# Layer 0's gated MLP: the seven-product form moves from the down projection to the up projection

## The chip, the cores and the metric

The kernel runs on one core of a Trainium2 chip. TensorE (PE in the profile) multiplies matrices into PSUM, which has eight banks of 128 x 512 float32. VectorE (DVE), ScalarE (ACT) and GpSimd (POOL) do the elementwise work; SyncE (SP) issues most of the loads. The metric is the device time in microseconds, the median of several runs; besides there is one profiled execution with its trace.

## The reference

Two decoder layers on 512 tokens of width 1024, all in float32. Layer 0 mixes tokens by causal pooling, layer 1 by sliding-window attention; each mixer is followed by a gated MLP with a causal convolution of width 3, and each has an RMS norm ahead of it. What matters here is the MLP of layer 0, with D_FF = 2816:

```python
def conv_glu_ffn(h, w_in, conv_w, conv_b, w_out):
    u = h @ w_in
    c = lax.conv_general_dilated(u, conv_w[:, None, :].astype(u.dtype), ..., feature_group_count=2 * D_FF) + conv_b
    a, g = c[..., :D_FF], c[..., D_FF:]
    return (a * jax.nn.silu(g)) @ w_out

hn = rms_norm(h, norm_ffn[i])
h = h + conv_glu_ffn(hn, ffn_w_in[i], ffn_conv_w[i], ffn_conv_b[i], ffn_w_out[i])
```

## The kernel before, in words

Activations lie with channels on partitions and tokens along the row: `h` is eight tiles of 128 x 512, and D_FF is 22 tiles of 128 channels. Every float32 product is made of three: each operand is split into a high part (a rounded copy, by ACT, line 99 for weights) and a low part (the rest, a subtraction on DVE, line 102), and `mm3` (lines 85 to 87) adds high x high, high x low and low x high in one bank. Weights come by `fetch` (line 91) into a `raw` tile (3 buffers) and are split into `wh` and `wl` tiles (4 buffers each).

The MLP of layer 0 is `mlp(fp, 0, ...)`, followed by `mlp_out`.

- Up (`mlp_in`): for each channel tile j and each s (1 is the gate g, 0 the value a), eight weight tiles of 128 x 128 times `xs` (the scaled `h` with the norm's gain, not yet its root) give one bank. There are six banks in this ring (`ps`) and two in the other (`aux`). The root of the norm is known late: the squares of `h` are added by `norm.add` (line 216, on POOL), `stats` multiplies by ones (line 222), `rsqrt_mean` finds the root on DVE, and `spread` brings it across partitions (line 233) into `rb` (line 236). So the first output tiles wait in their banks.
- `conv_chunk`: DVE multiplies the bank by `rb` into `c_u` (line 359), ACT makes the first tap with the bias (line 362), and two shifted adds follow on DVE (lines 363 and 364). The gate gets its Silu on ACT (line 402), and line 411 multiplies.
- Down: the 22 channel tiles are 11 pairs, in groups of 4, 4 and 3. The first two groups use a form with seven products for a 2 x 2 block product instead of eight (Winograd's variant of Strassen's): the blocks are the two channel tiles of a pair, two output tiles, and the two halves of 256 tokens. `split_sum` makes seven sums of the activations per pair; `sum_weights` makes seven weight tiles out of four, called R (two as loaded), Q (one as loaded), U (two sums, which an accumulating DMA from POOL's queue makes, line 460) and W (two further sums by POOL, lines 463 and 464); `mlp_sums` runs four rounds of seven products per group. A product is four channel tiles times three matmuls of 256 columns, so a round is 84 matmuls; it copies a bank's half out by ACT between two products (lines 483 and 487). The third group is plain (`mlp_out`): six channel tiles, three matmuls of 512 columns each, for each of eight output tiles; `after` then makes the scaled input of the attention and the squares for its norm.

The order on each engine is fixed when the program is built. A planner walks through the program with its own estimates of durations: on each engine it places, of what is ready, the instruction that stands first in program order. `pin` keeps chosen instructions in program order. Engines then run their lists in order, and waits are inserted where one needs another's result or a buffer.

Of the kernel before, what the change touches and what calls it, by code (L numbers as in the profile page):

```python
# [19 lines left out]
F32 = mybir.dt.float32  # L20
# [6 lines left out]
P = 128  # L27
D = 1024
# [8 lines left out]
GROUPS = (((4, True), (4, True), (3, False)), ((4, True), (4, True), (3, False)))  # L37
# [21 lines left out]
def trunk(ctx: ExitStack, tc: tile.TileContext, x_tok, x_t, vecs, w_pool, w_kq, w_v, w_o, w_in, gain, w_out, w_sums, w_tok, out):  # L59
# [48 lines left out]
    def in_weights(layer, j, s, eng=None, raw=None, pin=lambda ins: ins):  # L108
        return weights(w_in[layer, j, s], D, f"wi{layer}_{j}_{s}", eng, raw, 256 if eng else 1024, pin)

    def out_weights(layer, m):
        n = 2 * GROUPS[layer][-1][0]
        w = weights(w_out[layer][m], n * P, f"wo{layer}_{m}")
        return [part(w, k) for k in range(n)]
# [133 lines left out]
    def pool_mixer(norm, xs, ws):  # L248
# [59 lines left out]
        for i, (j, t) in enumerate(pre[:3]):  # L308
# [3 lines left out]
            raws.append(fetch(w_in[0, j, t], D, f"wi0_{j}_{t}"))  # L312
# [39 lines left out]
        for c in range(NC):  # L352
            norm.add(c)


# [11 lines left out]
    def mlp_in(fp, layer, xs, norm, ws0, z, turns):  # L367

        pairs = [k for n, k in GROUPS[layer] for _ in range(n)]
# [8 lines left out]
        for n, sums in GROUPS[layer]:  # L378
            first += 2 * n
            stops.add(min(first - 1 + sums, NF - 1))  # L380
# [67 lines left out]
    def sum_weights(fp, layer, g, p, n):  # L448

        src = w_sums[layer][g][p]  # L450
        w = n * P
        name = f"ws{layer}_{g}_{p}"
        v = fp.tile([P, 1024], F32, tag="uv", name=f"{name}_u_raw", bufs=4)
        u, v = v, fp.tile([P, 1024], F32, tag="uv", name=f"{name}_v_raw", bufs=4)
        r = wp.tile([P, 1024], F32, tag="raw", name=f"{name}_r_raw", bufs=3)
        q = wp.tile([P, 1024], F32, tag="raw", name=f"{name}_q_raw", bufs=3)
        nc.sync.dma_start(u[:, : 2 * w].rearrange("p (a b) -> p a b", a=2), src[:, 0:4:2, :])
        nc.sync.dma_start(r[:, : 2 * w].rearrange("p (a b) -> p a b", a=2), src[:, 0:2, :])
        nc.sync.dma_start(q[:, :w], src[:, 3, :])
        pin(G.dma_start(u[:, : 2 * w].rearrange("p (a b) -> p a b", a=2), src[:, 2:4, :], accum_op=ALU.add))  # L460
        R = weights(None, 2 * w, f"{name}_r", raw=r)
        Q = weights(None, w, f"{name}_q", raw=q)
# [590 lines left out]
```

## Time and profile before

| | us |
|---|---|
| runs before: median of 3 (lowest to highest) | 907.51 (907.15 to 907.55) |
| the profiled execution's own time | 907.31 |
| its span, first to last instruction | 905.6 |
| TensorE busy in the span | 895.2 |
| VectorE busy in the span | 683.2 |
| ScalarE busy in the span | 453.7 |
| GpSimd busy in the span | 192.3 |

The profile shows one execution. A row of its groups names the line, the engine, the operation, the output and inputs by the program's names, the shape and the count, then the busy time, the mean duration of one in ns, and the idle time of the engine before them with what ended most of it. A row of the timeline gives the start and the duration in us. Consecutive instructions of an engine overlap by their latency, so what one of them holds the engine for is the distance from start to start. A string of 40 digits shows the busy share in tenths, one for each fortieth of the span.

### The profile page before, as it was taken

The page shows a single profiled execution, that of the slowest core. Times are in us where ns is not written, and L with a number is a line of the kernel's source. Part 1 is how long each engine was busy: PE and PEld are TensorE (multiplying, and loading weights), DVE is VectorE, ACT ScalarE, POOL GpSimd, SP SyncE. Part 2 cuts the span into 40 slices and gives each one's busy share as a digit, 9 for nine tenths or more (in the row PEclk, how much of TensorE's full clock was granted, in tenths as well). Part 3 has the DMA queues.
Part 4 walks back from the last instruction along what each step waited for, and adds up shares of the span by engine and source line. Part 5 has one row for each costly group of instructions (what it writes and reads, how often), then busy time and mean ns, then how long its engine had stood idle before and what let it go on. Part 6 is the DMA issues. An engine that isn't in the chain of part 4 may idle for free.

```text
span 905.6 us, 12207 instructions
## 1 busy us (share of the span) xinstructions
PE 895.2 (99%) x4560; PEld 764.0 (84%) x4560; DVE 683.2 (75%) x1066; ACT 453.7 (50%) x697; POOL 192.3 (21%) x265
## 2 busy tenths in 40 slices
PE   9999999999999999999999999999999999999996
PEld 8888889888899888888889888888888888888885
DVE  7689998688987676555887381998976888966744
ACT  7755454444454344535888352654433444534434
POOL 3810123000321000425765040000230002300004
PEclk9999999999999999999999999999999999999999
DMA  8342536423444323322110041338286221453202
GB/s 321 114 139 93 152 86 189 134 98 106 122 116 134 124 69 93 117 94 93 48 47 24 1 162 48 117 122 227 48 219 197 94 93 47 93 173 107 93 24 93
DMA packets 30748, 101.29 MB, mean 112 GB/s; under 512 B 3296, under 2 KB 3296, under 8 KB 30688
## 3 DMA queue, kind: packets, MB, share of 16 engines
q1 hardware_dynamic: 28384, 92.11, 30.4%
q0 software_dynamic: 2304, 8.39, 5.5%
q8 instruction: 36, 0.59, 0.3%
q14 instruction: 24, 0.20, 0.1%
HBM read 98.39 MB, written 2.10 MB: 111 GB/s over the span
## 4 chain that ended last, share of the span: by engine, by line
PE 92%; POOL 3%; ACT 2%; DVE 1%; issue 1%; ACTq 0%; POOLq 0%; DVEq 0%
PE bank L85 29%; PE bank L86 29%; PE bank L87 29%; POOL wi_l L102 1%; PE bank L889 1%; PE bank L917 1%; POOL n_acc L216 1%; PE bank L288 1%; ACT sc L905 1%; PE bank L255 1%; PE bank L523 0%; PE bank L233 0%; PE bank L222 0%; ACT wo_h L99 0%; ACT px_h L243 0%
## 5 line engine op out<-in xcount | busy, mean ns | idle before, releaser
L99 ACT ACTIVATE wi_h<-wi_raw 128x1024 fp32r<-128x1024 f32 x88 | 93.1, 1061 | 144.1 <-PE bank L86 126.0
L102 DVE TENSOR_TENSOR wi_l<-wi_raw,wi_h 128x1024 fp32r<-128x1024 f32 x84 | 104.3, 1245 | 46.1 <-ACT wi_h L99 45.2
L85 PE MATMUL bank<-f1x_h,wi_h 128*128 128x512 f32 x352 | 137.9, 392 | 0.0
L87 PE MATMUL bank<-f1x_h,wi_l 128*128 128x512 f32 x352 | 137.1, 389 | 0.0
L86 PE MATMUL bank<-f1x_l,wi_h 128*128 128x512 f32 x352 | 137.0, 389 | 0.0
L86 PE MATMUL bank<-f0x_l,wi_h 128*128 128x512 f32 x352 | 137.0, 389 | 0.0
L87 PE MATMUL bank<-f0x_h,wi_l 128*128 128x512 f32 x352 | 136.9, 389 | 0.0
L85 PE MATMUL bank<-f0x_h,wi_h 128*128 128x512 f32 x352 | 136.5, 390 | 0.0
L359 DVE TENSOR_TENSOR c_u<-bank,n_rb 128x512 f32<-128x512 f32 x88 | 60.0, 687 | 45.5 <-PE bank L87 45.5
L364 DVE SCALAR_TENSOR_TENSOR c_t<-c_u,vec,c_t 128x510 f32<-128x510 f32 x88 | 76.5, 872 | 2.4
L87 PEld LDWEIGHTS bank<-f1x_h,wi_l 128*128 128x128 f32 x352 | 66.1, 188 | 13.9
L87 PEld LDWEIGHTS bank<-f0x_h,wi_l 128*128 128x128 f32 x352 | 66.1, 188 | 13.9
L85 PEld LDWEIGHTS bank<-f0x_h,wi_h 128*128 128x128 f32 x352 | 66.1, 188 | 13.6
L86 PEld LDWEIGHTS bank<-f1x_l,wi_h 128*128 128x128 f32 x352 | 66.1, 188 | 13.5
L85 PEld LDWEIGHTS bank<-f1x_h,wi_h 128*128 128x128 f32 x352 | 66.1, 188 | 13.5
L86 PEld LDWEIGHTS bank<-f0x_l,wi_h 128*128 128x128 f32 x352 | 66.1, 188 | 13.5
L362 ACT ACTIVATE c_t<-c_u,vec 128x512 f32<-128x512 f32 x88 | 70.3, 806 | 7.9 <-DVE c_u L359 7.1
L363 DVE SCALAR_TENSOR_TENSOR c_t<-c_u,vec,c_t 128x511 f32<-128x511 f32 x88 | 67.3, 769 | 0.1
L435 ACT ACTIVATE zh<-y 128x256 fp32r<-128x256 f32 (+2 forms) x44 | 37.9, 861 | 58.9 <-DVE y L411 51.1
L216 POOL TENSOR_TENSOR n_acc<-n_acc,n_sq 128x512 f32<-128x512 f32 x21 | 32.7, 1556 | 131.9 <-ACT n_sq L207 129.1
L402 ACT ACTIVATE c_t<-c_t 128x512 f32<-128x512 f32 x44 | 27.6, 628 | 60.0 <-DVE c_t L364 59.9
L437 DVE TENSOR_TENSOR zl<-y,zh 128x1536 fp32r<-128x1536 f32 (+2 forms) x36 | 41.9, 1165 | 9.4 <-ACT zh L435 9.1
(246 smaller groups left out, 2008.5 us busy)
## 6 DMA issues: line engine op xcount, KB each, us to landing
wi_raw<-w_in SPq DMA_DIRECT2D x88, 512.0 KB, 3.3
wt_a_raw<-w_tok SPq DMA_DIRECT2D x12, 512.0 KB, 4.7
kq_raw<-w_kq SPq DMA_DIRECT2D x10, 512.0 KB, 3.2
ws_u_raw<-w_sums SPq DMA_DIRECT2D x8, 512.0 KB, 4.7
ws_u_raw<-w_sums POOLq DMA_DIRECT2D x8, 512.0 KB, 5.5
ws_r_raw<-w_sums SPq DMA_DIRECT2D x8, 512.0 KB, 3.6
wo_raw<-w_o SPq DMA_DIRECT2D x8, 512.0 KB, 3.3
wt_s_raw<-w_tok SPq DMA_DIRECT2D x8, 512.0 KB, 5.5
```

What stands on the lines that cost most here:

```text
L85: T.matmul(ps, lhsT=wh, rhs=xh, start=start, stop=False, **kw)
L86: T.matmul(ps, lhsT=wh, rhs=xl, start=False, stop=False, **kw)
L87: T.matmul(ps, lhsT=wl, rhs=xh, start=False, stop=stop, **kw)
L99: pin(A.activation(h[:, :n], raw[:, :n], AF.Copy))
L102: (eng or V).tensor_tensor(l[:, o], raw[:, o], h[:, o].bitcast(F32), ALU.subtract)
L216: eng.tensor_tensor(self.acc[:, lo:hi], self.acc[:, lo:hi], sq[:, lo:hi], ALU.add)
L359: V.tensor_tensor(u, ps, rb, ALU.mult)
L362: A.activation(t, u, AF.Identity, bias=col(V_CB + layer * 2 * NF + m), scale=cw[2])
L363: V.scalar_tensor_tensor(t[:, 1:], u[:, : S - 1], cw[1], t[:, 1:], ALU.mult, ALU.add)
L364: V.scalar_tensor_tensor(t[:, 2:], u[:, : S - 2], cw[0], t[:, 2:], ALU.mult, ALU.add)
L435: A.activation(h, src, AF.Copy, scale=sign)
L437: V.tensor_tensor(l, src, h.bitcast(F32), ALU.subtract)
```

## The change

Layer 0's MLP becomes one function, `mlp_halves`. Layer 1 is not touched, except that its functions lose the `layer` argument.

- The first four channel tiles (`PLAIN = 4`, eight output tiles) are made as before, but `conv_sum` reads the bank itself: DVE multiplies it in place by `rb` (`late`), and ACT and the two shifted adds read the bank.
- After half of the fourth output tile, `sums()` makes seven sums of the scaled input with the full norm in it: channel tile p (0 to 3) with p + 4, and the two token halves. They are kept in `th` and `tl` for the rest of the layer. They are computed in tiles that the summed weights use later (`vh`, `vl`, `ur`).
- For j = 4 to 21 the value and the gate of j come from seven products of 256 columns, each over four channel pairs. The blocks are the two halves of the input channels, value and gate, and the token halves. `half_weights(j)` loads and sums the weights, with U and W in buffers of their own (`vh` and `vl`, 3 each; raw U in `ur`, 2). Three half banks are copied by ACT and three are combined by DVE in each step. The convolution needs no multiplication by `rb` any more. The last of the seven products is put off into the next step.
- Down is plain, in five groups of 4, 5, 5, 5 and 3 channel tiles. `down(g)` yields after each unit of three matmuls of 512 columns, and `fill(j, i)` threads such units between the products from j = 6 on, eight or nine per step; 46 units come after the last step. Each group adds its bank to `h`.
- The norm's squares are added on DVE instead of POOL. The finished `z` tiles take the buffers of `xs`.

```diff
+GROUPS = ((4, True), (4, True), (3, False))
+DOWN0 = (4, 5, 5, 5, 3)
+PLAIN = 4
...
-            norm.add(c)
+            norm.add(c, eng=V)
...
+    def conv_sum(fp, ps, m, name):
+        cw = [col(V_CW + t * 2 * NF + m) for t in range(3)]
+        t = fp.tile([P, S], F32, tag="t", name=f"{name}_t", bufs=4)
+        A.activation(t, ps, AF.Identity, bias=col(V_CB + m), scale=cw[2])
+        V.scalar_tensor_tensor(t[:, 1:], ps[:, : S - 1], cw[1], t[:, 1:], ALU.mult, ALU.add)
+        V.scalar_tensor_tensor(t[:, 2:], ps[:, : S - 2], cw[0], t[:, 2:], ALU.mult, ALU.add)
+        return t
...
+        def gated(j, ps):
+            gate[j] = conv_sum(fp, ps, NF + j, f"g{j}")
+            A.activation(gate[j], gate[j], AF.Silu)
+        def valued(j, ps):
+            t = conv_sum(fp, ps, j, f"a{j}")
+            V.tensor_tensor(t, t, gate.pop(j), ALU.mult)
...
+            A.activation(zh, t, AF.Copy)
+            V.tensor_tensor(zl, t, zh.bitcast(F32), ALU.subtract)
+            z.append((zh, zl))
+        def late(j, s, ps):
+            V.tensor_tensor(ps, ps, rb, ALU.mult)
+            (gated if s else valued)(j, ps)
...
+        def sums():
+            mx, px = (sm.tile([P, S], F32, tag="sq", name=f"{x}x") for x in "mp")
+            A.activation(mx[:, lo], rb[:, lo], AF.Copy, scale=-1.0)
+            A.activation(mx[:, hi], rb[:, hi], AF.Copy)
+            A.activation(px, mx, AF.Copy, scale=-1.0)
...
+            for p in range(4):
...
+                V.scalar_tensor_tensor(y[:, 0:4:3, :], h1, col(V_NFF + p), m2, ALU.mult, ALU.mult)
+                V.scalar_tensor_tensor(y[:, 1:3, :], h2, col(V_NFF + p + 4), p2, ALU.mult, ALU.mult)
+                V.tensor_tensor(v[:, 0, :], y[:, 3, :], y[:, 0, :], ALU.add)
+                V.tensor_tensor(y[:, 3, :], y[:, 3, :], y[:, 2, :], ALU.add)
+                V.scalar_tensor_tensor(v[:, 1, :], y[:, 2, :], -1.0, v[:, 0, :], ALU.mult, ALU.subtract)
+                V.tensor_tensor(v[:, 2, :], y[:, 1, :], v[:, 1, :], ALU.subtract)
+                for src, a, b in ((y, 0, 4), (v, 4, 7)):
...
+                    A.activation(hh, x, AF.Copy)
+                    V.tensor_tensor(ll, x, hh.bitcast(F32), ALU.subtract)
...
+        def half_weights(j):
...
+            nc.sync.dma_start(u2, src[:, 0:4:2, :])
+            nc.sync.dma_start(r2, src[:, 0:2, :])
+            nc.sync.dma_start(q[:, :n], src[:, 3, :])
+            pin(G.dma_start(u2, src[:, 2:4, :], accum_op=ALU.add))
+            R = weights(None, 2 * n, f"uw{j}_r", raw=r)
+            U = own_split(u, f"uw{j}_u")
+            G.tensor_tensor(r[:, :n], r[:, :n], u[:, n:], ALU.add)
+            G.tensor_tensor(r[:, n:], r[:, n:], r[:, :n], ALU.add)
+            W = own_split(r, f"uw{j}_v")
+            Q = weights(None, n, f"uw{j}_q", raw=q)
+            return R, U, W, Q
...
+        def down(g):
+            first, n = sum(DOWN0[:g]), DOWN0[g]
...
+            for m in range(NC):
+                ps = bank("aux")
+                for k in range(n):
+                    mm3(ps, w[k], z[first + k], k == 0, k == n - 1)
+                    if k == 0 and m + 1 < NC:
+                        ahead = load(m + 1)
+                    if k == n - 1:
+                        V.tensor_tensor(h[m], ps, h[m], ALU.add)
+                        if g == len(DOWN0) - 1:
+                            after(m)
+                    yield
+                w = ahead
...
+        for at in range(2, 2 * PLAIN):
+            w, ps = ahead, bank("ps")
+            if at + 1 < 2 * PLAIN:
+                ahead = load()
+            else:
+                ws = half_weights(PLAIN)
+            for k in range(NC):
+                if at == 3 and k == NC // 2:
+                    rb = norm.spread(bank("aux"), r)
+                    sums()
+                mm3(ps, part(w, k), xs[k], k == 0, k == NC - 1)
+            pend.append((*todo[at], ps))
+            if at == 2:
+                r = norm.stats(bank("aux"))
+            if rb is not None:
+                for x in pend:
+                    late(*x)
+                pend = []
...
+        for j in range(PLAIN, NF):
+            R, U, W, Q = ws
+            if j + 1 < NF:
+                ws = half_weights(j + 1)
+            ba, bx = bank("ps"), bank("ps")
...
+            product(ba[:, lo], R, 0, 0)
+            A.activation(s1, ba[:, lo], AF.Copy)
+            if last:
+                last()
+            fill(j, 0)
+            product(ba[:, lo], W, 0, 5, False)
+            A.activation(s2, ba[:, lo], AF.Copy, scale=-1.0)
+            product(bx[:, lo], R, 1, 1)
+            V.tensor_tensor(bx[:, lo], bx[:, lo], s1, ALU.subtract)
+            fill(j, 1)
+            product(ba[:, lo], U, 0, 3, False)
+            A.activation(s3, ba[:, lo], AF.Copy)
+            product(bx[:, hi], U, 1, 4)
+            V.tensor_tensor(ba[:, hi], bx[:, hi], s3, ALU.add)
+            fill(j, 2)
+            product(ba[:, lo], Q, 0, 6, False)
+            gated(j, ba)
+            def last(j=j, bx=bx, W=W, s2=s2):
+                product(bx[:, hi], W, 1, 2, False)
+                V.tensor_tensor(bx[:, hi], s2, bx[:, hi], ALU.subtract)
+                valued(j, bx)
+            fill(j, 3)
+        last()
+        for x in fills:
+            pass
```

More of the change, by code (lines that the diff above doesn't have):

```diff
@@ L58, in trunk @@
 @with_exitstack
-def trunk(ctx: ExitStack, tc: tile.TileContext, x_tok, x_t, vecs, w_pool, w_kq, w_v, w_o, w_in, gain, w_out, w_sums, w_tok, out):
+def trunk(ctx: ExitStack, tc: tile.TileContext, x_tok, x_t, vecs, w_pool, w_kq, w_v, w_o, gain, w_in, w_half, w_down, w_end, w_tok, out):
     nc = tc.nc
@@ L108, in in_weights @@
     def in_weights(layer, j, s, eng=None, raw=None, pin=lambda ins: ins):
[L109 to L114, printed above, removed]
+        return weights(w_in[layer][j, s], D, f"wi{layer}_{j}_{s}", eng, raw, 256 if eng else 1024, pin)
     pin = tc.keep_in_program_order
@@ L367, in mlp_in @@
     def mlp_in(fp, layer, xs, norm, ws0, z, turns):
-        pairs = [k for n, k in GROUPS[layer] for _ in range(n)]
+        pairs = [k for n, k in GROUPS for _ in range(n)]
         todo = [(j, s) for j in range(NF) for s in (1, 0)]
@@ L377, in mlp_in @@
         stops, first = set(), 0
-        for n, sums in GROUPS[layer]:
+        for n, sums in GROUPS:
             first += 2 * n
@@ L446, in plain @@
         return res
[L448 to L462, printed above, removed]
-        G.tensor_tensor(v[:, :w], u[:, w : 2 * w], r[:, :w], ALU.add)
-        G.tensor_tensor(v[:, w : 2 * w], v[:, :w], r[:, w : 2 * w], ALU.add)
-        W = weights(None, 2 * w, f"{name}_v", raw=v)
-        U = weights(None, 2 * w, f"{name}_u", raw=u)
-        return R, Q, W, U
@@ L499, in mlp @@
-    def mlp(fp, layer, xs, norm, ws0=None):
+    def mlp(fp, xs, norm):
         z, ht = [], []
-        up = mlp_in(fp, layer, xs, norm, ws0, z, turned(fp, ht) if layer else iter(()))
+        up = mlp_in(fp, 1, xs, norm, None, z, turned(fp, ht))
         done, first = 0, 0
-        for g, (n, sums) in enumerate(GROUPS[layer]):
+        for g, (n, sums) in enumerate(GROUPS):
             upto = first + 2 * n
@@ L508, in mlp @@
             zg = z[first // 2 : upto // 2]
-            if sums and layer:
+            if sums:
                 mlp_tokens(g, zg, ht)
-            elif sums:
-                mlp_sums(fp, layer, g, n, zg)
             first = upto
@@ L690, in mlp_end @@
         store(NT - 1)
-    def mlp_out(layer, z, after):
-        for m in range(NC):
-            w = out_weights(layer, m)
-            ps = bank("ps")
-            for k in range(len(z)):
-                mm3(ps, w[k], z[k], k == 0, k == len(z) - 1)
-            V.tensor_tensor(h[m], ps, h[m], ALU.add)
-            after(m)
     norm0, norm1, norm2 = (Norm(f"n{i}") for i in range(3))
@@ L1043 @@
     args = {k: nc.dram_tensor(k, v.shape, mybir.dt.from_np(v.dtype), kind="ExternalInput").ap() for k, v in arrays.items()}
[L1044 to L1045 removed]
+    w_in = [args.pop(f"w_in{i}") for i in range(2)]
+    w_half = args.pop("w_half")
+    w_down = [args.pop(f"w_down{g}") for g in range(len(DOWN0))]
+    w_end = args.pop("w_end")
     w_tok = [[args.pop(f"w_tok{g}{x}") for x in range(len(SETS[g]))] for g in range(len(SETS))]
```

144 lines of the change are left out of this document (91 added, 53 removed).

## The prediction, made before the change was run

> **What bounds the kernel now.** I read the head of the page, the list of waits for TensorE, and then stretches.
>
> ```profile
> span 905.6 us, 12207 instructions
> PE 895.2 (99%) x4560; PEld 764.0 (84%) x4560; DVE 683.2 (75%) x1066; ACT 453.7 (50%) x697; POOL 192.3 (21%) x265
> DVE  7689998688987676555887381998976888966744
> PE 92%; POOL 3%; ACT 2%; DVE 1%; issue 1%; ACTq 0%; POOLq 0%; DVEq 0%
> ```
> ```profile
> PE bank L255 <- DVE warm L253: 2.2, 1, 2.2
> PE bank L222 <- POOL n_acc L216: 0.2, 1, 0.2
> ```
>
> TensorE (PE) is busy 99% of the span, 92% of the chain that ended last is its own work, and it waited twice, for 2.4 us together. So removing matrix work can pay in full, and any new wait of PE is paid in full too. VectorE (DVE) averages 75%, but its digits are 8 and 9 in the slices of layer 0's up projection. This window inside it, before the first down group, shows how little is free:
>
> ```profile
> 59.00:97.00 38.00, 38.00 (x169) 31.49 (x168) 37.72 (x55) 23.94 (x31) 0.00 (x0) 1.00 0.26 81
> 126.99:137.06 10.07, 10.07 (x85) 10.07 (x84) 9.86 (x14) 5.88 (x9) 1.42 (x2) 1.00 0.59 145
> ```
>
> The columns are PE, weight load, DVE, ACT and POOL. DVE works 37.72 of 38.00 us there, clearing the convolutions that pile up before the norm is known. A change that adds DVE work at that place has nothing to hide it in.
>
> **The matrix work.** Matmul durations overlap, so I count from start to start. The second window row above is one round of the old sums: 84 products of 256 columns in 10.07 us, 120 ns each. For 512 columns:
>
> ```profile
> 317.83 0.39 PE L85 MATMUL bank<-f0x_h,wi_h 128*128 128x512 f32 x1
> ...
> 331.88 0.39 PE L87 MATMUL bank<-f0x_h,wi_l 128*128 128x512 f32 x1
> ```
>
> These are 62 steps in 14.05 us: 227 ns.
>
> Up: 18 of the 22 output pairs change from 48 products of 512 (10.88 us) to seven times 12 of 256 (10.07), so 18 x 0.81 = 14.6 us are saved, not the eighth that the count promises: 120 is more than half of 227. Down: two groups lose the form. Each had four rounds of 10.07 and now costs 192 products of 512, 43.5 instead of 40.3; two groups add 6.5. Net **-8.1 us**, with the same forms of instruction as before, so this I hold to within 1 us.
>
> **The start, where the change moves the most.** Today DVE multiplies a bank by the norm into `c_u`, which frees the bank. After, `conv_sum` reads the bank itself, so a bank stays taken until both shifted adds on it are done. There are six banks. And `sums()` stands ahead of all eight convolutions of the plain tiles in program order. Prices on DVE, start to start:
>
> ```profile
> 62.01 0.74 DVE L363 SCALAR_TENSOR_TENSOR c_t<-c_u,vec,c_t 128x511 f32<-128x511 f32 x1
> 62.67 0.68 DVE L359 TENSOR_TENSOR c_u<-bank,n_rb 128x512 f32<-128x512 f32 x1
> 63.27 0.74 DVE L364 SCALAR_TENSOR_TENSOR c_t<-c_u,vec,c_t 128x510 f32<-128x510 f32 x1
> 63.92 0.68 DVE L411 TENSOR_TENSOR y<-c_t,c_t 128x512 f32<-128x512 f32 x1
> 64.53 1.28 DVE L359 TENSOR_TENSOR c_u<-bank,n_rb 128x512 f32<-128x512 f32 x2
> 65.72 0.42 DVE L437 TENSOR_TENSOR zl<-y,zh 128x256 fp32r<-128x256 f32 x1
> 66.06 1.41 DVE L363 SCALAR_TENSOR_TENSOR c_t<-c_u,vec,c_t 128x511 f32<-128x511 f32 x2
> ...
> 73.40 2.35 DVE L102 TENSOR_TENSOR wi_l<-wi_raw,wi_h 128x1024 fp32r<-128x1024 f32 x2
> ```
> ```profile
> L99 ACT ACTIVATE wi_h<-wi_raw 128x1024 fp32r<-128x1024 f32 x88 | 93.1, 1061 | 144.1 <-PE bank L86 126.0
> ```
>
> So 0.66 for a three-operand instruction of 512 columns, 0.60 for two operands, 0.34 for 256 columns, 1.18 for 1024, and 0.89 for 768 as three quarters of that. `sums` per channel pair: 2 x 0.66 + 4 x 0.34 + 1.18 + 0.89 = 4.75, four pairs **19.0 us** without a gap, since four pairs have eight buffers and ACT needs only two splits per pair (1.06 and three quarters of it, 1.9 us). A late gate costs 0.60 + 2 x 0.66 = 1.92, a late value 1.92 + 2 x 0.60 = 3.12; eight of them **20.2**. PE then has four plain tiles left, 4 x 24 x 0.227 = 21.8 us; DVE has 39.
>
> When does it begin?
>
> ```profile
> 26.75 0.62 PE L85 MATMUL bank<-f0x_h,wi_h 128*128 128x512 f32 x2
> 48.90 1.05 PE L222 MATMUL bank<-ones,n_acc 128*128 128x2 f32 x8 [0.23 <-POOL n_acc L216]
> 49.81 0.48 PE L85 MATMUL bank<-f0x_h,wi_h 128*128 128x512 f32 x1
> ```
> ```profile
> 37.62 11.23 POOL L216 TENSOR_TENSOR n_acc<-n_acc,n_sq 128x512 f32<-128x512 f32 x7
> ```
> ```profile
> 32.29 3.37 DVE L244 SCALAR_TENSOR_TENSOR f0x_l<-h,vec,f0x_h 128x512 fp32r<-128x512 f32 x3 [0.78 <-ACT f0x_h L243]
> 50.10 1.22 DVE L102 TENSOR_TENSOR wi_l<-wi_raw,wi_h 128x1024 fp32r<-128x1024 f32 x1
> ```
> ```profile
> 56.45 0.60 ACT L236 ACTIVATE n_rb<-bank 128x512 f32<-128x512 f32 x1
> ```
>
> The seven squares' adds leave POOL, where they ended at 48.85 and held the statistics, for DVE, which is free from 35.66: 7 x 0.60 = 4.2, done by about 40. So the statistics now follow the third tile: 26.75 + 72 x 0.227 = 43.1. From there to `n_rb` took 8.15 us (48.90 to 57.05) with two weight splits of 1.2 in between; without them 5.8. So `n_rb` at 48.9 to 51.2, and after ACT's signed copies `sums` begins at about 50.3 and ends at **69.3**. PE, with 0.9 for the statistics (48.90 to 49.81) and as much for the spread, ends the fourth tile at 50.3, the fifth at 55.8, the sixth at 61.2. The seventh needs a bank, the one of the first: its multiply may fit before `sums`, its two shifted adds (1.3) come behind it, 70.6. **PE waits 9.4 us** (8 if `sums` begins at 49).
>
> The eighth tile's weight split and the splits of j=4 stand behind the convolutions 0 to 3 (10.1, less the 1.3 above and two early multiplies, 7.5), and j=4's summed weights behind `ur` buffers that `sums` holds to its end:
>
> ```profile
> ws_u_raw<-w_sums SPq DMA_DIRECT2D x8, 512.0 KB, 4.7
> ws_u_raw<-w_sums POOLq DMA_DIRECT2D x8, 512.0 KB, 5.5
> L463 POOL TENSOR_TENSOR ws_v_raw<-ws_u_raw,ws_r_raw 128x512 f32<-128x512 f32 x8 | 13.5, 1686 | 162.2 <-DMA ws_r_raw<-w_sums 133.9 <-DVE c_u L359 7.8 <-DVE ws_u_l L102 6.2
> L464 POOL TENSOR_TENSOR ws_v_raw<-ws_v_raw,ws_r_raw 128x512 f32<-128x512 f32 x8 | 13.1, 1633 | 0.6
> ```
>
> The buffer comes free at 68.4, before the last split of `sums`: 68.4 + 4.7 + 5.5 + 1.7 + 1.6 + 2.2 of splits = 84, while PE could begin j=4 at 70.6 + 2 x 5.44 = 81.5. j=4 and j=5 have no down work threaded in. I add 3.1 us there (0 to 9, by whether the split slips into gaps or waits for all convolutions): **+12.5** together.
>
> A long wait may cost once more, in the clock:
>
> ```profile
> 2.23 5.76 PE L255 MATMUL bank<-warm 128*128 128x144 f32 x24 [2.23 <-DVE warm L253]
> 7.83 2.37 PE L288 MATMUL bank<-sband,xt 128*128 128x144 f32 x18
> ```
>
> After idle time at the start PE ran 240 ns apart, later 122, at equal width. If 9 us of waiting bring that back, half of 5.76 us is lost; I take 1.5 (0 to 2.9). The Trainium skill, "TensorE: Matmul & The Clock Gate", Part 1, says that the array falls to half rate after an idle window of about 3.4 us and needs a busy one to recover; by it I estimate 1.7, and the start of this trace agrees in kind, though its granted clock reads 1.00.
>
> **The loop from j=6 to 21.** PE per step: 10.07 plus eight units of down work at 3 x 0.227, 15.5. DVE: 3.5 splits (4.1), four shifted adds 2.6, two of 512 1.2, three of 256 1.0, and 1.6 down tiles at 0.74 + 0.60 = 2.1; together 11.1. ACT has fewer and shorter passes. DVE has 4.4 us free, so the engines keep up. A step loads 1.79 MB and 1.6 tiles of 0.33, 149 GB/s, about the 145 of the old round above, and that round never starved. What is new are round trips in one bank: five of PE to ACT or DVE and back per step. The shortest cover is between the product of U with t=4 and that of Q: two units, 1.36 us, against 0.42 of DVE work behind at most one split (1.18). I take 0.15 a step, **+2.4** (0 to 16). POOL's sums share that time:
>
> ```profile
> L102 DVE TENSOR_TENSOR ws_u_l<-ws_u_raw,ws_u_h 128x1024 fp32r<-128x1024 f32 x8 | 11.3, 1407 | 0.0
> L102 DVE TENSOR_TENSOR ws_v_l<-ws_v_raw,ws_v_h 128x1024 fp32r<-128x1024 f32 x8 | 9.8, 1231 | 1.3 <-ACT ws_v_h L99 1.0
> ```
>
> U's splits, which can meet them, averaged 0.18 us more than those of the finished sum, which can't; that changes nothing. The Trainium skill, "SBUF — State Buffer", section "SBUF: two separate sides", has the two engines lock each other out for whole instructions; by it DVE could lose both POOL adds, 3.3 us a step by the rows, which I estimate at 4 us more in j=4 and 5 and nothing later. The trace's 0.18 speaks against that, so it stays out of the sum.
>
> **The end.** 46 units stay behind the loop, 31 us of PE; the last group takes 2.04 us per output tile, and the squares' adds on POOL 1.6 (11.23 / 7). Nothing new is late, and it costs 0.
>
> Sum: -8.1 + 12.5 + 1.5 + 2.4 = **+8.3 us**. The profiled execution took 907.31 us, 1.7 more than its span and 0.2 less than the median of the three runs; so **915.6**.
>
> **Rivals.** Faster: the start is hidden, because DVE takes convolutions between the pieces of `sums` or works them quicker than priced. Against it: if the first four convolutions go first, they and `sums` still hold 19.0 + 10.1 + 2.4 (two splits) from 49.5, so j=4 begins at 81 instead of 72. It decides the sign when all waits of PE stay under 6.3 us. With 2 us of waits: 907.3 - 8.1 + 2 = **901.2**. Worse in the loop: four weight buffers serve R, Q and down tiles, a down tile holds one for five units (10 us) with the next one loaded ahead, and a split that gets no buffer keeps its raw tile, with SP's later loads queued behind it, until PE waits, say, for one 1024-column split (1.06 us) a step, 16 instead of 2.4: **929**. For it: ACT idled 126.0 us before splits of `wi_h` until PE gave buffers back; against: none of that reached PE. That the form saves nothing in the up projection can nearly be excluded, as the same 256-column products ran at 120 ns.
>
> **How the numbers follow.** About 0.2% (1.8 us) can be told from no change. The forecast's own range is 909 to 923, chance 0.53; worse in the loop 0.14; faster 0.24; waits and saving cancelling 0.09. So slower 0.67, same 0.09, faster 0.24. The range 901 to 927 takes in the faster case's middle and leaves most of the worst out.
>
> **What would show it.** After: PE's list of waits has the seventh plain tile waiting 8 to 11 us for DVE at 61 us; DVE is full from 50 to 90; the rounds of 84 still take 10.07 us of PE; waits after j=6 are below 0.5 us each. Wrong if PE has no wait over 3 us before 90 us, or if the loop's waits exceed the start's.

## The result and the profile after

| | before | after |
|---|---|---|
| median of four runs each, us | 907.49 | 948.85 |
| lowest to highest | 907.15 to 907.55 | 947.36 to 949.77 |
| span of the profiled execution | 905.6 | 948.1 |

The ratio is 1.0455 (95% interval 1.0437 to 1.0473). The sign was forecast; the time lies 33 us above the forecast and 22 above its range.

The head of the page of after, with PE's busy share and the granted clock (PEclk) in tenths:

```profile
span 948.1 us, 13258 instructions
PE 903.6 (95%) x4920; PEld 779.7 (82%) x4920; DVE 704.3 (74%) x1127; ACT 483.0 (51%) x782; POOL 221.2 (23%) x288
PE   8976799999989999999999999999999999999996
PEclk9986899999999999999999999999999999999999
```

The third to fifth digits of the PE row (47 to 118 us) fell to 7, 6 and 7, and the clock row dips at the same place. TensorE's waits of 1 us and more behind the warm-up (total, times, longest, in us):

```profile
PE bank L89 <- DVE wi_l L104: 8.0, 1, 8.0
PE bank L87 <- ACT th L414: 7.0, 1, 7.0
PE bank L87 <- DVE bank L535: 5.8, 5, 1.5
PE bank L87 <- ACT sn L523: 5.7, 1, 5.7
PE bank L87 <- DVE bank L530: 2.6, 4, 1.1
PE bank L87 <- ACT sn L528: 2.2, 3, 0.9
PE bank L87 <- DVE h L463: 1.3, 1, 1.3
PE bank L219 <- DVE n_acc L213: 1.0, 1, 1.0
```

There are three single waits of 6 to 8 us and some thirteen smaller ones of up to 1.5 us. The ledger of the lost time comes from the trace: I take every distance between the starts of two neighbouring TensorE instructions, subtract the undisturbed pitch of the form (the distance from start to start in a stream: 227 ns for 512 columns, 120 for 256, and likewise for the smaller ones), and add up by stretch. The planner moves some products of one step in among those of the next, so the steps are told apart by count: 2 x 84 products of 256 columns belong to j=4 and j=5. By that count j=6 begins at 125.1 us, and the last product of j=21 starts at 391.1. What is over the pitch is called excess below.

| us | predicted | after less before |
|---|---|---|
| fewer products | -8.1 | -8.1 |
| ahead of 40 us | 0 | -0.5 |
| 40 us to j=6, with the clock | +14.0 | +33.0 |
| loop, j=6 to 21 | +2.4 | +16.1 |
| behind the loop | 0 | +2.2 |
| sum | +8.3 | +42.7 (spans: +42.5) |

The saving came as computed. Seven products run at the priced pitch:

```profile
97.28 0.28 PE L89 MATMUL bank<-th,uw_r_l 128*128 128x256 f32 x1
...
98.00 0.28 PE L89 MATMUL bank<-th,uw_r_l 128*128 128x256 f32 x1
```

Six steps take 0.72 us, 120 ns each. So two questions are left: why the start cost 19 us more than forecast, and the loop 14.

**The start.** Windows of after; the columns are PE, weight load, DVE, ACT, POOL (busy us and count), then granted clock, DMA share and GB/s:

```profile
26.75:63.50 36.75, 35.78 (x159) 29.21 (x157) 31.08 (x56) 22.76 (x32) 9.39 (x9) 0.95 0.24 79
63.50:71.00 7.50, 0.48 (x2) 0.30 (x2) 7.50 (x16) 3.90 (x5) 0.00 (x0) 0.70 0.00 0
71.00:80.00 9.00, 8.95 (x28) 6.95 (x28) 9.00 (x14) 5.16 (x7) 1.04 (x1) 0.68 0.56 146
80.00:88.50 8.50, 0.54 (x3) 0.34 (x3) 5.65 (x9) 3.54 (x5) 0.00 (x0) 0.71 0.16 30
98.00:104.00 6.00, 0.40 (x4) 0.19 (x2) 1.57 (x3) 1.96 (x4) 1.68 (x2) 0.72 0.75 204
```

In the second row PE stands still while DVE is busy for the whole of it: this is the seventh plain tile's wait for a bank. The list puts it down to ACT's `th`, which that product doesn't read. What it needs is the bank, and the timeline of DVE in after has the last instruction on it, the second shifted add, which ends 0.15 us before PE goes on at 70.73 (in a later run, with part of the sums on GpSimd, the list itself names this add, with 8.1 us):

```profile
52.84 0.74 DVE L406 SCALAR_TENSOR_TENSOR ty<-h,vec,mx 128x512 f32<-128x512 f32 x1
...
69.84 0.74 DVE L359 SCALAR_TENSOR_TENSOR g_t<-bank,vec,g_t 128x510 f32<-128x510 f32 x1
...
73.88 0.95 DVE L415 TENSOR_TENSOR tl<-ty,th 128x768 fp32r<-128x768 f32 x1
...
83.91 0.75 DVE L358 SCALAR_TENSOR_TENSOR g_t<-bank,vec,g_t 128x511 f32<-128x511 f32 x1 [2.85 <-ACT g_t L357]
...
87.16 1.22 DVE L104 TENSOR_TENSOR wi_l<-wi_raw,wi_h 128x1024 fp32r<-128x1024 f32 x1
```

The first and third lines are the first and last of `sums`, 52.84 to 74.8; in between DVE slips in one multiplication and four shifted adds. The last line is the eighth tile's weight split, for which PE stood from 80.4 to 88.4. The 2.85 us of idle DVE at 83.91 belong to ACT's queue, shown here in after:

```profile
82.15 1.06 ACT L419 ACTIVATE uw_u_h<-uw_u_raw 128x1024 fp32r<-128x1024 f32 x1 [3.48 <-DMA uw_u_raw<-w_half]
83.12 0.76 ACT L357 ACTIVATE g_t<-bank,vec 128x512 f32<-128x512 f32 x1
...
102.04 1.06 ACT L419 ACTIVATE uw_u_h<-uw_u_raw 128x1024 fp32r<-128x1024 f32 x1 [5.75 <-DMA uw_u_raw<-w_half]
...
103.67 0.37 ACT L523 ACTIVATE sn<-bank 128x256 f32<-128x256 f32 x1
```

Twice ACT stands with the split of U at the head of its queue, waiting for U's accumulating load; the convolution's first tap (line 357) and the copy that PE needs (line 523) are ready behind it. POOL's timeline shows why the second of these loads is late:

```profile
90.86 1.59 POOL L437 TENSOR_TENSOR uw_r_raw<-uw_r_raw,uw_u_raw 128x512 f32<-128x512 f32 x1 [13.37 <-DVE uw_r_l L104]
92.53 2.15 POOL L438 TENSOR_TENSOR uw_r_raw<-uw_r_raw 128x512 f32<-128x512 f32 x1
94.63 0.89 POOL L434 DMA_DIRECT2D uw_u_raw<-w_half  x1
```

The load for j=5 is issued from POOL's queue, right behind the two additions for j=4, and these waited until 90.86 for DVE's split of R. So the wait of 5.7 us comes by the order in POOL's queue.

**The clock.** The third window row has 28 products of 512 columns in 9.00 us; at 0.227 they need 6.36. Just after the stall they are 0.42 apart:

```profile
71.72 0.63 PE L89 MATMUL bank<-f0x_h,wi_l 128*128 128x512 f32 x1
72.14 0.63 PE L87 MATMUL bank<-f0x_h,wi_h 128*128 128x512 f32 x1
```

So the stalls are paid once more: between 40 us and j=6 the waits make 23.2 of the 33.4 us of excess, slow pitch nearly all the rest. The first window row, with its 0.95, shows that the clock also dipped once before the first long wait: from 46.0 to 49.5 us it was granted by half, and eight products were 0.42 us apart.

**The loop.** One of its waits in after, on POOL, DVE and PE:

```profile
266.44 1.60 POOL L437 TENSOR_TENSOR uw_r_raw<-uw_r_raw,uw_u_raw 128x512 f32<-128x512 f32 x1 [17.70 <-DVE uw_r_l L104]
```
```profile
265.08 1.22 DVE L104 TENSOR_TENSOR uw_r_l<-uw_r_raw,uw_r_h 128x1024 fp32r<-128x1024 f32 x1
...
266.81 1.78 DVE L383 TENSOR_TENSOR z13l<-a_t,z13h 128x512 fp32r<-128x512 f32 x1
268.51 0.42 DVE L535 TENSOR_TENSOR bank<-bank,sn 128x256 f32<-128x256 f32 x1
```
```profile
268.99 0.39 PE L87 MATMUL bank<-th,uw_q_h 128*128 128x256 f32 x1 [1.27 <-DVE bank L535]
```

DVE's subtraction in line 383 takes 0.68 us elsewhere; here, beside POOL's addition, it took 1.78. The addition that PE needs (line 535) starts that much later, and PE waits 1.27. In the loop of after 14 DVE instructions beside POOL's additions are 0.36 to 1.10 us longer than their like, 12.1 together. Seven of the loop's twelve waits, 7.2 of 9.3 us, come within 4.2 us behind one that was held up by 0.78 or more; four times it stands directly in front of the addition that PE waits for (line 530 or 535).

### The profile page after: what moved, and what is told of

Same layout as the page of the kernel before. It is cut to its first block, busy times and chain, and to the rows that moved or that the text cites. A ratio compares the mean times of both kernels' runs of the same rounds, so it can differ in the third digit from the quotient of the medians.

```text
span 948.1 us, 13258 instructions
## 1 busy us (share of the span) xinstructions
PE 903.6 (95%) x4920; PEld 779.7 (82%) x4920; DVE 704.3 (74%) x1127; ACT 483.0 (51%) x782; POOL 221.2 (23%) x288
## 4 chain that ended last, share of the span: by engine, by line
PE 56%; DVE 2%; ACT 2%; POOL 1%; issue 1%; DMA 1%; ACTq 0%; POOLq 0%; DVEq 0%
PE bank L87 18%; PE bank L89 18%; PE bank L88 17%; PE bank L1021 1%; PE bank L1049 1%; POOL n_acc L213 1%; ACT sc L1037 1%; DMA uw_u_raw<-w_half 1%; PE bank L664 0%; DVE h L463 0%; DVE ax_l L241 0%; POOL vl L867 0%; ACT q L932 0%; PE bank L219 0%; PE bank L230 0%
## 5 line engine op out<-in xcount | busy, mean ns | idle before, releaser
L101 ACT ACTIVATE wi_h<-wi_raw 128x1024 fp32r<-128x1024 f32 x52 | 54.9, 1060 | 86.8 <-PE bank L88 70.0
L104 DVE TENSOR_TENSOR wi_l<-wi_raw,wi_h 128x1024 fp32r<-128x1024 f32 x48 | 58.6, 1225 | 30.5 <-ACT wi_h L101 29.7
L87 PE MATMUL bank<-th,uw_v_h 128*128 128x256 f32 x144 | 41.4, 287 | 5.7 <-ACT sn L523 5.7
L87 PE MATMUL bank<-th,uw_u_h 128*128 128x256 f32 x144 | 41.5, 288 | 4.8 <-DVE bank L530 2.6
L89 PE MATMUL bank<-th,uw_v_l 128*128 128x256 f32 x144 | 41.3, 287 | 0.0
L88 PE MATMUL bank<-tl,uw_v_h 128*128 128x256 f32 x144 | 41.3, 287 | 0.0
L87 PE MATMUL bank<-th,uw_r_h 128*128 128x256 f32 x144 | 40.8, 283 | 0.1
L88 PE MATMUL bank<-tl,uw_r_h 128*128 128x256 f32 x144 | 40.8, 284 | 0.0
L88 PE MATMUL bank<-tl,uw_u_h 128*128 128x256 f32 x144 | 40.7, 283 | 0.0
L89 PE MATMUL bank<-th,uw_u_l 128*128 128x256 f32 x144 | 40.7, 282 | 0.0
```

Source lines behind the costliest of these rows:

```text
L87: T.matmul(ps, lhsT=wh, rhs=xh, start=start, stop=False, **kw)
L88: T.matmul(ps, lhsT=wh, rhs=xl, start=False, stop=False, **kw)
L89: T.matmul(ps, lhsT=wl, rhs=xh, start=False, stop=stop, **kw)
L101: pin(A.activation(h[:, :n], raw[:, :n], AF.Copy))
L104: (eng or V).tensor_tensor(l[:, o], raw[:, o], h[:, o].bitcast(F32), ALU.subtract)
```

## The experiments

Two theories. **Backlog:** the start is DVE's amount of work (`sums` and eight convolutions against four plain tiles); the loop's waits come from GpSimd's additions for W, which hold DVE up. **Banks and queues:** the start is the place of single things (a bank kept taken, the eighth tile's split, the buffers and loads of U); the loop's waits come from the short round trips, or from the weight buffers. Runs without an interval are single executions; after's own runs lie 2.4 us apart, so I read nothing into less than 2 us.

### Without the two additions

```diff
-            G.tensor_tensor(r[:, :n], r[:, :n], u[:, n:], ALU.add)
-            G.tensor_tensor(r[:, n:], r[:, n:], r[:, :n], ALU.add)
```

> Leaves out GpSimd's two additions per step that make the weights W (W is then a copy of R, so what these products add is wrong); nothing else. Theory lock (an addition on GpSimd holds up a VectorE instruction with two SBUF inputs by about 1.1 us, and what PE waits for stands behind it): PE's waits for lines 530 and 535, now 8.4 us after 104 us, fall under 3, and the time falls by 7 to 10 us to about 940. Rival cover (the round trip through VectorE is too long for two units of down work whatever GpSimd does): those waits stay above 6 and the time falls by less than 3 us. The two long waits before 90 us stay in both.

Measured: 927.24, span 925.5, with W a copy of R. The loop's excess fell from 16.3 to 3.9 us (by the ledger's method), the wait of 5.7 is gone, those of 7.0 and 8.0 (now 8.6) stay. The waits at lines 530 and 535 went as the theory of the lock expects, but the gain is twice what I expected. The larger part, 12.4 us, is in the loop, 9.9 in the start. POOL's additions, and what waits for them, cost about 20 us, though they never appear as a releaser in after's list for PE.

### The plain banks freed early

```diff
-            V.tensor_tensor(ps, ps, rb, ALU.mult)
-            (gated if s else valued)(j, ps)
+            u = fp.tile([P, S], F32, tag="u", name=f"u{j}_{s}", bufs=2)
+            V.tensor_tensor(u, ps, rb, ALU.mult)
+            (gated if s else valued)(j, u)
```

> The late multiplication by the norm writes to SBUF (two buffers) and not back into the bank, as in the kernel before. Theory bank (the seventh plain tile waits only because its bank is held until two shifted adds behind sums are done): the wait of 7.0 us at 63 us goes. Since VectorE's work is the same, theory backlog expects the next wait, for the eighth tile's weights, to grow by as much less the clock's part: time 944 to 948. If order of work and not its amount counts, 938 to 941.

Measured: 942.63. The single wait of 7.0 became 3.8 and 2.6, the next fell to 3.5, and later ones grew (2.7 at the line that copies `sn`). Up to the start of j=4 the excess fell by 7.4 us; 1.4 of it was lost again by j=6. Less than the wait that went; the time lies between the two expected ranges and decides for neither.

### U loaded early

```diff
-            tag, bufs = (("vh", 3), ("vl", 3), ("ur", 2))[min(i // 3, 2)]
+            tag = "vl" if i % 6 // 3 else "vh"
```

The tiles of `sums` no longer use U's raw buffers.

> The temporaries of sums use only the vh and vl buffers, so the raw buffers of U are free and their loads can start 25 us sooner. Theory head of queue (ScalarE's list holds U's split, which waits for the accumulating load, and what VectorE and PE need stands behind it): PE's wait for the copy of line 523 (5.7 us at 98 us) goes, the wait for the eighth tile's weights (8.0 us) gets 3 us shorter, and the time falls by 8 to 11 us to about 939. Theory backlog (VectorE simply has too much to do before 100 us): the waits shift but their sum falls by less than 3 us.

Measured: 942.18. The wait for the eighth tile's split fell from 8.0 to 5.0 as expected; the one at line 523 stayed (6.2), and the start's waits fell by 3.0 us in all. The load for j=5 was issued at 90.05, again right behind POOL's two additions. Without the additions it was issued at 77.33, with them on VectorE (below) at 79.70, and there the waits at this line are 0.6 us and none. So the late load was due to POOL's queue, and not to the buffers.

### The eighth tile's split on GpSimd

```diff
-        load = lambda: ws0.pop(0) if ws0 else in_weights(0, *todo[at + 1])
+        load = lambda: ws0.pop(0) if ws0 else in_weights(0, *todo[at + 1], G if at + 1 == 7 else None)
```

> The low part of the eighth plain tile's weights is made on GpSimd, which idles from 38 to 76 us, and not on VectorE. Theory order (that split stands behind eight others in VectorE's list although its inputs have been there since 55 us): the wait of 8.0 us at 80 us goes, the raw buffer comes free earlier, so R of j=5 is loaded earlier; a part comes back as a wait for j=4's W; time down by 5 to 9 us to about 942. Theory backlog: the wait only moves to j=4's products, down by less than 2 us.

Measured: 947.35, no gain above the spread of after. The wait of 8.0 is gone, the first grew to 9.2, and the total at line 528 grew from 2.2 to 6.7, while that at line 523 fell from 5.7 to 3.0. That is what the backlog expects, but the run is not clean: beside GpSimd's split, four instructions of `sums` took about 0.5 us longer each, 2.1 together, which is how much the first wait grew.

### The additions made but not used

```diff
-            G.tensor_tensor(r[:, :n], r[:, :n], u[:, n:], ALU.add)
-            G.tensor_tensor(r[:, n:], r[:, n:], r[:, :n], ALU.add)
+            k = fp.tile([P, 1024], F32, tag="k", name=f"uw{j}_k", bufs=1)
+            G.tensor_tensor(k[:, :n], r[:, :n], r[:, n:], ALU.add)
+            G.tensor_tensor(k[:, n:], r[:, n:], k[:, :n], ALU.add)
```

> GpSimd makes two additions of the same size per step, but from R alone and into a tile that nobody reads; W is again a copy of R (those products are wrong). So GpSimd's work is there and nothing waits for its result. Theory lock (the additions stop VectorE): the waits at lines 530 and 535 after 104 us come back to 5 to 9 us and VectorE shows instructions lengthened by 1.1 us; time 934 to 940. Rival chain (W's split waits for the additions, which wait for R's split and U's load, and stands in front of what PE needs): the time stays near the 927.2 of the run without additions, within 2 us.

Measured: 934.13, 7 above the run without additions and 15 below after. The time lies in the range that I had expected from the lock, but not by its mechanism: the 7 us are in the start (6.2 of them between 40 us and j=6), and the waits at lines 530 and 535 did not come back. In the loop DVE is still held up (13 instructions, 8.8 us together), but the ledger's excess there is 3.7 us: the delays now fall where PE doesn't wait. So holding DVE up isn't enough; it must strike just ahead of what PE needs.

### The additions on VectorE

```diff
-            G.tensor_tensor(r[:, :n], r[:, :n], u[:, n:], ALU.add)
-            G.tensor_tensor(r[:, n:], r[:, n:], r[:, :n], ALU.add)
+            V.tensor_tensor(r[:, :n], r[:, :n], u[:, n:], ALU.add)
+            V.tensor_tensor(r[:, n:], r[:, n:], r[:, :n], ALU.add)
```

> The two additions per step run on VectorE, 1.2 us more work for it per step, and none on GpSimd; everything is computed. Theory lock: the loop's waits fall although VectorE has more to do; time 934 to 941. Rival chain: W's split waits for U's load and the additions as before, now in VectorE's own list, so the loop's waits stay or grow: 946 to 955.

Measured: 931.69, 17 us less than after and somewhat under the range of the lock; the rival is out. TensorE's longest waits behind the warm-up:

```profile
PE bank L89 <- DVE wi_l L104: 7.7, 1, 7.7
PE bank L87 <- ACT th L414: 7.0, 1, 7.0
PE bank L87 <- DVE h L463: 1.3, 1, 1.3
```

The waits for lines 523 to 535 are gone, and no DVE instruction of the loop is lengthened. DVE does 36 instructions of 0.68 more, 24 us of busy time, and the whole is 17 us shorter. The ledger: 25.0 in the start, 5.8 in the loop, so the additions on GpSimd cost 8.4 and 10.5. In the start they held DVE up for only 2.0 us; the 8.4 are mostly the wait of 5.7 for the load behind them, with the slow products that follow it. What round trips and pitch cost by themselves in the loop is 5.6 more than before.

### The three together, and the convolutions first

The first kernel has the three edits above (banks freed, U early, additions on VectorE). The second also moves `sums()` behind the first four late convolutions:

```diff
-                    sums()
...
+            if at == 3:
+                sums()
```

> Sums of weights on VectorE, bank freed by the late multiplication, U's buffers free from the start. If the three causes are separate, the gains add: about 6 + 6 + 8 below 947.4, 925 to 930. If they are one backlog on VectorE, 934 to 940. The kernel before is not reached in either, since VectorE has about 39 us to do while PE has 22 us of plain tiles left.

> As the one with the three together, and sums is issued after the first four convolutions. Theory order: PE's waits before the eighth plain tile vanish and the ones at j=4 grow by less, 3 to 6 us faster than the three together. Theory backlog: the same time within 2 us, since the same 39 us of VectorE stand before j=4's first product.

Measured: 926.87 and 926.88. The order of DVE's work changed nothing, though the picture did: the first has waits of 3.8, 3.5, 2.6 and 2.2, the second has all of it in one. The second's timelines, DVE and PE:

```profile
83.00 1.21 DVE L104 TENSOR_TENSOR wi_l<-wi_raw,wi_h 128x1024 fp32r<-128x1024 f32 x1
```
```profile
84.27 0.79 PE L89 MATMUL bank<-f0x_h,wi_l 128*128 128x512 f32 x1 [14.88 <-DVE wi_l L104]
```

That is what a backlog looks like: whichever job comes last, PE waits for the amount. The time of the first run, though, lies in the range that I had given to separate causes. That range was added up from gains of 6, 6 and 8, and the third brought 17.2; the gains measured one by one, 6.2, 6.7 and 17.2, make 30, and the three together brought 22. So they overlap, as one backlog would have it, without that proving it.

### The additions on GpSimd, not in place

```diff
-            G.tensor_tensor(r[:, :n], r[:, :n], u[:, n:], ALU.add)
-            G.tensor_tensor(r[:, n:], r[:, n:], r[:, :n], ALU.add)
-            W = own_split(r, f"uw{j}_v")
+            k = fp.tile([P, 1024], F32, tag="k", name=f"uw{j}_k", bufs=1)
+            G.tensor_tensor(k[:, :n], r[:, :n], u[:, n:], ALU.add)
+            G.tensor_tensor(k[:, n:], r[:, n:], k[:, :n], ALU.add)
+            W = own_split(k, f"uw{j}_v")
```

> GpSimd's two additions are those of the change, with their results used, but they write a tile of their own instead of R's raw tile, so they can start when the loads have landed and don't wait for VectorE's split of R. Theory place (each addition starts when the split of R ends and so hits the next VectorE instruction, just ahead of what PE waits for): the waits at lines 530 and 535 after 130 us, 7 us or so, fall under 2, with as much lengthening on VectorE as before; time 934 to 942. Rival lock alone (any addition on GpSimd costs PE about the same): waits and time stay, 945 to 949.

Measured: 932.47, within 1 us of the additions on VectorE and a little under the range expected if the place counts; the other theory is out. Its timelines, POOL and DVE:

```profile
178.46 1.28 POOL L438 TENSOR_TENSOR uw_k<-uw_r_raw,uw_u_raw 128x512 f32<-128x512 f32 x1 [11.79 <-DVE uw_v_l L420]
179.82 1.30 POOL L439 TENSOR_TENSOR uw_k<-uw_r_raw,uw_k 128x512 f32<-128x512 f32 x1
```
```profile
179.91 2.29 DVE L104 TENSOR_TENSOR uw_r_l<-uw_r_raw,uw_r_h 128x1024 fp32r<-128x1024 f32 x1 [1.54 <-ACT uw_r_h L101]
```

DVE loses 1.07 us here as well (1.22 elsewhere), but in a weight split with time to spare. In place, the first addition overwrites R, so it starts when DVE's split of R ends (the releaser `uw_r_l` above, 15 of 18 times in after) and strikes DVE's next instructions, which in this loop are those ahead of PE. With its own tile it starts earlier, released by another split. The loop's excess is 5.8, the same as with VectorE, although DVE is still held up there for about 7.5 us in all (12.1 in after). The start's excess fell from 33.4 to 26.3, since the load for j=5, behind the additions in POOL's queue, is now issued at 83.52.

### Part of the sums on GpSimd

The additions on VectorE and U loaded early, and besides:

```diff
-                    V.tensor_tensor(ll, x, hh.bitcast(F32), ALU.subtract)
+                    (G if p > 1 else V).tensor_tensor(ll, x, hh.bitcast(F32), ALU.subtract)
```

> Everything is computed: weight sums on VectorE, U's buffers free, and the low parts of the last two of the four channel pairs in sums on GpSimd, 4.1 us less for VectorE at the start; the convolutions read the bank as in the change. Theory backlog: PE's waits before 100 us are shorter by about 4 than with the weight sums on VectorE and U's buffers free alone; time 920 to 924. Rival lock: what VectorE saves it loses again to instructions held up by GpSimd: 926 to 930. Still slower than the kernel before, by 1.5 to 2.5%.

Measured: 930.09, ratio to before 1.0256 (1.0239 to 1.0273), at the upper end of what the lock lets expect and far from the backlog's 920 to 924. Taking four of `sums`' low parts off DVE brought nothing that can be told from 931.69, because DVE was held up again, in `sums` itself:

```profile
66.17 1.91 DVE L409 TENSOR_TENSOR ty<-ty 128x256 f32<-128x256 f32 x1
68.00 2.02 DVE L410 SCALAR_TENSOR_TENSOR ty<-ty,ty 128x256 f32<-128x256 f32 x1
...
70.60 1.91 DVE L411 TENSOR_TENSOR ty<-ty,ty 128x256 f32<-128x256 f32 x1
```

These take 0.41 to 0.42 us otherwise. The three lose 4.6 us, while POOL is busy with the low parts. And U's loads, free to start early by the second edit, were issued at 75.26 only, behind these low parts in POOL's queue.

### Without the late multiplication

The kernel with the convolutions first, less the multiplication of the eight plain tiles by `rb`.

```diff
-            u = fp.tile([P, S], F32, tag="u", name=f"u{j}_{s}", bufs=2)
-            V.tensor_tensor(u, ps, rb, ALU.mult)
-            (gated if s else valued)(j, u)
+            (gated if s else valued)(j, ps)
```

> As the one with the convolutions first, but the eight plain tiles are not multiplied by the norm (their convolutions are wrong by that factor): 8 x 0.60 = 4.8 us less for VectorE, four of the eight before the eighth tile's weight split, and each convolution starts one step sooner. Theory backlog (PE's wait at the start is VectorE's work counted out): the long wait of 14.9 us falls by 2.4 to 4.8, time down by 3 to 5 from 926.9 to about 923. Rival (a latency, not an amount, sets the wait): within 1 us of 926.9.

Measured: 924.73, 2.2 less, where 3 to 5 were expected. The convolutions no longer wait for `rb`, so they moved ahead of the statistics and pushed `sums` to 59 us: the run changes two things and decides little.

### The sums left out

From the kernel with the additions on VectorE:

```diff
-                tl.append(fp.tile([P, 7, HS], F32R, tag="tl", name=f"tl{p}", bufs=4))
...
+                tl.append(th[p])
+                for i, c in ((0, p), (2, p + 4), (4, p)):
+                    A.activation(th[p][:, i : i + 2, :].rearrange("p a b -> p (a b)"), h[c], AF.Copy)
+                A.activation(th[p][:, 6, :], h[p + 4][:, lo], AF.Copy)
```

> As the kernel with both weight additions on VectorE (931.69 us), but the input sums are left out: the up projection's products run on plain copies of h that ScalarE makes, seven blocks per channel pair as before, and serve as both parts, so VectorE does nothing for them (the result is not the layer's). VectorE's backlog in the start falls from about 39 us to 20 beside TensorE's 21.8 us of plain tiles. If that backlog is the whole cost of the start: the waits of 7.7 and 7.0 go, with the half-rate stretches behind them, 19 to 25 us less, 907 to 912. If the form saves what the prediction's 8.1 us say and nothing else of the start is late, 899 to 903, the time of the faster rival. Rival, the bank theory (the eighth tile's split, the loads of U and the head of ScalarE's queue cost on their own): at least one wait over 4 us stays before 110 us, and it ends over 914.

Measured: 909.96 (907.62 to 911.24), ratio to before 1.0035 (1.0023 to 1.0048), in the range expected if the backlog is the whole cost of the start. Waits of TensorE over 0.5 us, between the warm-up and the second layer:

```profile
PE bank L87 <- ACT sn L514: 1.5, 2, 1.1
PE bank L87 <- DVE h L454: 1.3, 1, 1.3
PE bank L87 <- DVE bank L521: 0.7, 1, 0.7
```

and two windows, from the start of the late convolutions to that of j=4, and on to j=6:

```profile
50.00:72.00 22.00, 22.00 (x99) 18.22 (x98) 21.89 (x32) 15.12 (x23) 0.00 (x0) 1.00 0.17 60
72.00:94.00 22.00, 20.86 (x166) 19.90 (x165) 19.24 (x28) 12.33 (x19) 1.72 (x2) 1.00 0.72 195
```

No wait over 1.3 us is left and the clock stays at 1.00; the start's excess is 2.6 instead of 25.0 us, the span 24.1 shorter. The eighth tile's split and the in-place banks are as they were, and cost nothing once DVE has 19 us less to do. U's first loads are not: without `sums` their buffers are free, and both are issued at 37.7 us. But the two runs of the three edits together issued them as early (38.4 and 38.6) and still had 20 us of excess in the start, so it is not these loads that make the difference. DVE is still busy for 21.89 of 22 us, so a full engine alone is no loss; one with more work than PE has beside it is. The last term is instructive: even with `sums` free the change gains nothing. The saving of 8.1 goes against 8.6 us of excess above before's: 2.2 in the start, 4.6 in the loop, 2.2 behind it, -0.4 ahead of 40 us. That is the ledger of the profiled execution, the fastest of the six with 907.62; the median's further 2.3 us are not explained.

## Why the prediction was right or wrong

- **The matrix work, -8.1:** right. The pitch held, and the ledger closes with it within 0.2 us.
- **The seventh plain tile "waits 9.4 us":** right in mechanism and nearly in size. `sums` began at 52.84 instead of 50.3 (the statistics had a wait of 1.0 and `n_rb` was ready at 51.6), a pair took 4.7 us without the work slipped in, and PE waited 7.0, from 63.5 instead of 61.2: it came later by the statistics' wait and by 1.4 us that the slow products from 46.0 to 49.5 us lost. The bank came at 70.6, to the tenth as computed. That is luck: `sums` began later, and the shifted adds slipped in before its end.
- **"I add 3.1 us there (0 to 9, ...)":** the first failed term. It measured 8.0 for the eighth tile's split, 5.7 and 1.5 in j=4 and j=5, together 15. I computed a backlog of 39 us against 21.8 of PE, a difference of 17.2, and then let only 12.5 of it become waiting, because splits might slip into gaps. They hardly did: with the additions on VectorE the start's waits add up to 16.8, nearly the whole difference, and in the run with the convolutions first 14.9 of it stands as one wait. Leaving `sums` out removed the waits, moving things about did not. The rest of after's 23.2 came with GpSimd's additions, the wait of 5.7 above all. That wait has a cause of its own, which the prediction doesn't have: U's accumulating load stood behind the additions in POOL's queue, and the prediction's sum for U's path, 68.4 + 4.7 + 5.5 and so on, stops at j=4.
- **The clock, "I take 1.5 (0 to 2.9)":** too small, since I priced one stall. Between 40 us and j=6 the trace of after has half the clock granted four times: from 46.0 to 49.5 us, 66.5 to 76.8, 83.6 to 93.8 and 100.7 to 107.5. The steps begun in these stretches lost 1.4, 2.9, 2.6 and 1.6 us against the pitch, 8.5 of the 10.2 us that are not waits. The Trainium skill, "TensorE: Matmul & The Clock Gate", Part 1, says that the array is at half rate after about 3.4 us of idling and at full rate again after as long of sustained work. The last three stretches agree in kind: each begins 2.3 to 3.1 us into a stall of 6 to 8, PE worked for 6.0, 5.4 and 3.4 us before the full clock came back, and in the run without `sums`, with no such stall, the windows have 1.00. The first doesn't agree: ahead of it PE had waited for 1.0 us only and run eight products of two columns, and in the run with the convolutions first the same wait left the clock at 1.00.
- **The loop, "+2.4 (0 to 16)":** the second failed term, with 16.1 just past the end of its range. The place was right: the shortest cover, between U's t=4 and Q, is line 535 and has the most waits. Round trips and pitch cost 5.6, GpSimd's additions 10.5. The step that failed is "The trace's 0.18 speaks against that, so it stays out of the sum". It took an average over eight instructions, of which two had been held up by 0.76 us each, as evidence that none are. Single rows of before showed it, here on DVE and POOL:

```profile
240.77 1.78 DVE L363 SCALAR_TENSOR_TENSOR c_t<-c_u,vec,c_t 128x511 f32<-128x511 f32 x1
242.59 1.67 DVE L364 SCALAR_TENSOR_TENSOR c_t<-c_u,vec,c_t 128x510 f32<-128x510 f32 x1
```
```profile
239.89 2.12 POOL L463 TENSOR_TENSOR ws_v_raw<-ws_u_raw,ws_r_raw 128x512 f32<-128x512 f32 x1 [7.85 <-DVE c_u L359]
242.08 1.62 POOL L464 TENSOR_TENSOR ws_v_raw<-ws_v_raw,ws_r_raw 128x512 f32<-128x512 f32 x1
```

  Shifted adds of 0.74 took 1.78 and 1.67, ended only after POOL's additions did, and PE, which then ran plain tiles of the up projection without round trips, never noticed. The Trainium skill, "SBUF — State Buffer", section "SBUF: two separate sides", says that a DVE instruction with two SBUF inputs and a GpSimd instruction that reads SBUF exclude each other for a whole instruction. These rows agree, and so does the run with part of the sums on GpSimd. The estimate that I made by this rule, 4 us in j=4 and 5 and nothing later, misplaced the cost too: I took DVE's 4.4 us of free time per step as cover. I had looked only for which work is hit, not where in DVE's queue: free time elsewhere in the step covers nothing when PE waits for the very next instruction. In place, hold-ups of 12.1 us cost PE 10.5; with a tile of its own, hold-ups of 7.5 us cost it nothing that the ledger shows.
- **The end, 0:** 2.2, most of it one wait of 1.3 at 420 us for a down tile's addition. A DVE instruction just ahead of it took 1.78 instead of 0.74 beside POOL's addition of squares, so it looks like the same hold-up; no run took that addition away.
- **The rivals.** "Worse in the loop", 929, had the better size for the loop but not the cause: its four weight buffers are the same in the kernel with additions on VectorE, where splits of weights hold PE up for about 2 us in all. "Faster", 901.2, can't be had from the start alone: with `sums` left out altogether the time is 909.96, since the loop's round trips and the end take the saving back.
- **What would show it:** the pitch came out. The wait at 61 us came at 63.5, with 7.0 us under the 8 to 11 named. DVE was full from 51.6 to 81 us and then stood for 2.85, so not quite from 50 to 90. "Waits after j=6 are below 0.5 us each" did not come out: they go up to 1.3.

No version reached the time of before; the best that leaves no work out, two orders of the same edits, took 926.9. What stays open is why the clock fell at 46 us, and a kernel in which `sums` is spread over the first two steps was not tried.

## What to carry to other kernels

When moved work meets an engine that is already full, price the whole difference between its backlog and the cover, then the clock on top for every stall; rearranging it only changes the name of the wait. Before putting an elementwise job on GpSimd beside a busy VectorE, look in the trace for single instructions of twice their usual length, not at means, and see what they stand in front of. An in-place operation is released by the last reader of its operand, so it can be nailed to the worst moment; a tile of its own for the result was worth 16 us here, some 10 of them in the loop. The rest has to do with another queue: a load that is issued from an engine's queue waits for the arithmetic ahead of it there.

## What the runs showed of the hardware

- A VectorE instruction with two SBUF inputs was held up by as much as 1.10 us beside one GpSimd addition of 128 x 512 (1.28 us by itself), and by 1.5 to 1.6 us beside a GpSimd subtraction of up to 1024 columns. GpSimd's additions grew too, from 1.26 to 2.16 us.
- After stalls of 6 to 8 us, products of 512 columns ran 0.42 us apart instead of 0.227, for 3.4 to 6.0 us; three such stretches lost 7.1 us. Once the clock halved for 3.4 us after a wait of only 1.0.
- ACT's queue head waiting for an accumulating load (512 KB, median 6.9 us from issue to landing, 5.5 before) stood for 3.5 and 5.75 us with ready work behind it. The second of these loads was issued at 94.63 from GpSimd's queue, behind two additions; without them ahead, at 77.33.
